# adaLN's later modulation vectors: transposed half rows of w_ada, multiplied with silu(c) and summed in one VectorE operation, in place of column sums that a matmul finishes

## The chip, the cores and the metric

The kernel runs on one core of a Trainium2 chip. The metric is the device time of one execution in microseconds (us); lower is better. The core's engines work in parallel, each through its own queue in order: TensorE (PE: matmuls, and their weight loads as PEld), VectorE (DVE), ScalarE (ACT), GpSimd (POOL), and SyncE (SP), whose queue issues every DMA of this kernel.

## The reference, cut to what matters

One layer of a hybrid encoder over a sequence of 1024 tokens with 1024 features, in float32. A conditioning vector `c` gives six modulation vectors, of which four are needed late: the gate of the attention part, shift and scale of the MLP part, and the gate of the MLP part.

```python
c_act = jax.nn.silu(c)                      # (1, 1024)
mod = c_act @ w_ada + b_ada                 # w_ada (1024, 6 * 1024)
shift_mix, scale_mix, gate_mix, shift_ffn, scale_ffn, gate_ffn = jnp.split(mod, 6, axis=-1)
h = modulate(rms_norm(x), shift_mix, scale_mix)          # h * (1 + scale) + shift
qa, ka, va, qb, kb, vb = jnp.split(h @ w_in, cuts, axis=-1)
oa = chunked_rel_attention(qa, ka, va, rel_bias)         # 8 heads
ob = stick_breaking_attention(qb, kb, vb)                # 8 heads
mixed = jnp.concatenate([rms_norm(oa) * g_a, rms_norm(ob) * g_b], axis=-1) @ w_out
x = x + gate_mix * mixed
h = modulate(rms_norm(x), shift_ffn, scale_ffn)
gate, val = jnp.split(causal_depthwise_conv(h @ w_up, conv_w, conv_b), 2, axis=-1)
x = x + gate_ffn * ((jax.nn.silu(gate) * val) @ w_down)
return rms_norm(x) * final_g
```

## The kernel before

Matrix products run as three matmuls each on a high and a low part of both operands (tiles ending in h and l); making the parts is work for ScalarE (the high part), VectorE and GpSimd (the low part, a subtraction).

The program has these stages. **Setup**, to about 75 us: the first two modulation vectors (`ada_sum`, with the features on the partitions), the modulated input `hT`, the first query and key products. **Attention**, to about 645 us: 128 units, each one head's 128 queries; units 0 to 63 are stick-breaking (pairs 0 to 3), units 64 to 127 chunked (pairs 4 to 7). A unit runs scores (matmuls `S`), weights (stick-breaking: ScalarE's sigmoids, a VectorE scan over `kt`, a GpSimd multiplication into `pb`; chunked: VectorE's maxima, ScalarE's exponential, a GpSimd scaling), transposes (matmuls `T`), the split of the transposed weights (ScalarE `pth`, VectorE `ptl`), and the product with the values (`pv`, again a `T` tile). Scores run two units ahead (`AHEAD`). Between the pieces `fill` puts matmuls `mm` of a list of jobs: the later projections and, at the end, the output projection of the stick-breaking half (`job_out_b`), which reads `w_out` and the first gate. **Output projection of the chunked half and the MLP** follow to the end.

The four later vectors are the generator `mods`, advanced once per unit from unit `MOD0` on. It takes 128 tiles `rawm` of 128 input features by 256 output features; a VectorE operation multiplies a tile with the 128 values of silu(c) that stand on its partitions and adds it to `macc`. After eight tiles the 128 partitions remain to be summed: `mod_out` does that with a matmul against ones, into a PSUM buffer of the tag "T" that attention uses too. The gates come out as a row and go through DRAM (`gate_d`), from which `load_gate` spreads them over all partitions; shift and scale come out as columns (`modv`).

The order in each queue is set by a scheduler, which places an instruction where its engine seems free, with the program's order as priority. TensorE's instructions of attention are pinned by `pe` (line 136) to the program's order, so that a matmul of `mod_out` holds its place among the others; the mods' VectorE operations and loads are not pinned. `BUFS` gives the buffers of each tag: `rawm` has 4 of 128x256, `macc` 1.

Of the kernel before, what the change touches and what calls it, by code (L numbers as in the profile page):

```python
# [11 lines left out]
F32 = mybir.dt.float32  # L12
# [35 lines left out]
MOD0 = 60  # L48
# [7 lines left out]
def build(nc, tc, t, ctx):  # L56
# [3 lines left out]
    def mk(pool, shape, dt, tag):  # L60
        cnt[0] += 1
        return pool.tile(shape, dt, name=f"{tag}_{cnt[0]}", tag=tag, bufs=BUFS.get(tag, 1))
# [16 lines left out]
    rev_d = mk(dr, [8, P, ULEN], F32, "revd")  # L79

# [54 lines left out]
    def pe(fn, *a, **k):  # L135
# [7 lines left out]
    smask = mk(pq, [P, P], F32, "smask")  # L143
    gp.memset(smask, 0.0)
    gp.affine_select(out=smask, in_=smask, pattern=[[-1, P]], compare_op=ALU.is_gt,
                     fill=NEG, base=0, channel_multiplier=1)
    smaskr, identr = (mk(pq, [P, P], F32R, n) for n in ("smaskr", "identr"))
    gp.tensor_copy(smaskr, smask)
# [63 lines left out]
    def new_k(pr):  # L212
        pr.kh = [mk(pq, [P, S], F32R, "kh") for _ in range(2)]
# [4 lines left out]
    ada = t["ada0"]  # L218
    sh_mix = mk(p0, [P, KB], F32, "sh_mix")
# [235 lines left out]
    sy.dma_start(rev_d, bass.AP(t["rev"].tensor, 0, [[ULEN, 8], [0, P], [1, ULEN]]))  # L455
    new_k(pairs[0])
# [88 lines left out]
    def job_out_b(_):  # L545
# [10 lines left out]
        bc = mk(p1, [P, S + 1], F32, "kt")  # L556
        load_gate(bc[:, 0:D])
# [331 lines left out]
    QC = 256  # L889

    def mods():


        seq = [(i, qt, kb) for i in MODS for qt in range(D // QC) for kb in range(KB)]
        tiles = {}

        def load(n):
            if n < len(seq):
                i, qt, kb = seq[n]
                tiles[n] = mk(p1, [P, QC], F32, "rawm")  # L900
                sy.dma_start(tiles[n], t["ada"][i - 2, kb, :, qt * QC:(qt + 1) * QC])

        load(0)
        load(1)
        yield
        for n, (i, qt, kb) in enumerate(seq):
            cols = i in (3, 4)
            if n % 2 == 0:
                load(n + 2)
                load(n + 3)  # L910
            w = tiles.pop(n)
            if kb == 0:
                if cols and qt == 0:
                    modv[i] = mk(p0, [P, KB], F32, f"mod{i}")
                acc = mk(p1, [P, QC], F32, "macc")
                ve.tensor_scalar(acc, w, cact[:, 0:1], None, ALU.mult)
            else:
                ve.scalar_tensor_tensor(acc, w, cact[:, kb:kb + 1], acc, ALU.mult, ALU.add)  # L918
            if kb == KB - 1:
                mod_out(i, qt, acc, cols)  # L920
            if n % 2:
                yield

    def mod_out(i, qt, acc, cols):
        mp = mk(ps1, [P, HALF], F32, "T")
        if cols:
            for b in range(2):
                pe(te.matmul, mp[:, b:b + 1], acc[:, b * P:(b + 1) * P], ones[:, 0:1], start=True, stop=True)
            k0 = 2 * qt
            ve.scalar_tensor_tensor(modv[i][:, k0:k0 + 2], mp[:, 0:2], 0.0 if i == 3 else 1.0,  # L930
                                    bada[:, 8 * i + k0:8 * i + k0 + 2], ALU.add, ALU.add)
        else:
            pe(te.matmul, mp[:, 0:QC], ones, acc, start=True, stop=True)
            bb = mk(p1, [1, QC], F32, "rawm")
            sy.dma_start(bb, bass.AP(t["b_ada"].tensor, i * D + qt * QC, [[QC, 1], [1, QC]]))
            ve.tensor_add(acc[0:1], mp[0:1, 0:QC], bb)
            sy.dma_start(gate_d[i // 5:i // 5 + 1, qt * QC:(qt + 1) * QC], acc[0:1])
# [583 lines left out]
```

## Time and profile before

| | |
|---|---|
| three runs | 1421.34, 1426.35, 1428.23 us; median 1426.35 us |
| profiled execution | 1425.51 us; its span, first to last instruction, 1423.5 us |
| TensorE busy | 1309.2 us (92% of the span) |
| VectorE busy | 1176.2 us (83%) |
| GpSimd busy | 864.9 us (61%) |
| ScalarE busy | 617.2 us (43%) |

Times in the views are from the span's start. Busy shares are averages over stages that differ; a stage is read by its own rows. In the views, L918 is line 918 of the kernel, `out<-in` names the tiles written and read, and "who waited" puts a wait down to the event that came last.

### The profile page before, as it was taken

To read this page: it belongs to the slowest core of one execution; us is meant where nothing else is said; L and a number is where in the kernel's file an instruction comes from. 1 tells how busy PE (TensorE), PEld (TensorE's weight loads), DVE (VectorE), ACT (ScalarE), POOL (GpSimd) and SP (SyncE) were. 2 spreads that over 40 slices of the span, in tenths; PEclk is the share of its full clock that TensorE was granted. 3 is DMA by queue.
4 is the path that set the end of the run, shared out by engine and by line. 5 is a ranking of instruction groups with operands and counts; after the bars stand their busy time and mean duration, and the time that the engine had idled before them with its cause. 6 is when DMAs were issued, how large, how long until landed. Compare 5 with 4: busy or idle time off the path is not lost.

```text
span 1423.5 us, 19845 instructions
## 1 busy us (share of the span) xinstructions
PE 1309.2 (92%) x6644; PEld 1083.0 (76%) x6644; DVE 1176.2 (83%) x1967; ACT 617.2 (43%) x1270; POOL 864.9 (61%) x760
## 2 busy tenths in 40 slices
PE   4889999999899978798887999999999999999996
PEld 2688998898778966676665877777777778777774
DVE  7858777677778868876889889999998889899887
ACT  5647567575545433333432333323333333333334
POOL 4646576765333436563578667776676677667664
PEclk9999999999999999899998999999999999999998
DMA  8534433414665686665011111111111111211213
GB/s 311 180 100 112 104 88 85 119 49 120 166 167 144 179 263 197 217 193 193 22 45 36 47 52 45 45 45 60 52 54 58 45 45 45 60 52 49 62 37 119
DMA packets 80047, 144.57 MB, mean 102 GB/s; under 512 B 10041, under 2 KB 36809, under 8 KB 79946
## 3 DMA queue, kind: packets, MB, share of 16 engines
q1 hardware_dynamic: 79946, 143.31, 33.9%
q8 instruction: 53, 0.87, 0.3%
q14 instruction: 48, 0.39, 0.1%
HBM read 102.89 MB, written 18.88 MB: 86 GB/s over the span
## 4 chain that ended last, share of the span: by engine, by line
PE 43%; DVE 35%; ACT 7%; issue 5%; DMA 5%; POOL 4%; SPq 1%; POOLq 0%; DVEq 0%; ACTq 0%
PE mm L136 14%; PE up L1128 12%; DVE y L1137 8%; PE T L136 6%; PE dnf L136 6%; DVE x L1262 4%; PE S L136 3%; ACT y L1133 3%; DVE ah L1071 3%; DVE y L1070 2%; DVE adaw L254 1%; DVE macc L918 1%; PE up L1302 1%; POOL wl L121 1%; DVE al L1072 1%
## 5 line engine op out<-in xcount | busy, mean ns | idle before, releaser
L1262 DVE TENSOR_TENSOR x<-dnf,x 128x512 f32<-128x512 f32 x340 | 222.5, 679 | 1.6 <-PE dnf L136 1.6
L1137 DVE SCALAR_TENSOR_TENSOR y<-y,sm,y 128x512 f32<-128x512 f32 (+2 forms) x160 | 187.3, 1171 | 28.8 <-ACT y L1133 28.7
L1128 PE MATMUL up<-h,wh 128*128 128x512 f32 x640 | 199.7, 393 | 2.6 <-ACT y L1170 1.8
L1094 POOL TENSOR_TENSOR wl<-raw,wh 128x1024 fp32r<-128x1024 f32 (+1 forms) x62 | 160.1, 2583 | 66.1 <-ACT wh L1092 59.5
L1133 ACT ACTIVATE y<-y,sm 128x512 f32<-128x512 f32 x80 | 65.3, 817 | 254.7 <-DVE y L1209 133.4
L136 PE MATMUL mm<-H,wh 128*128 128x512 f32 x448 | 150.2, 403 | 0.0
L1128 PEld LDWEIGHTS up<-h,wh 128*128 128x128 f32 x640 | 119.7, 189 | 31.1 <-ACT y L1170 5.2
L136 PE MATMUL dnf<-dh,ah 128*128 128x512 f32 x336 | 133.5, 397 | 10.0 <-DVE x L1262 8.8
L136 PE MATMUL dnf<-dl,ah 128*128 128x512 f32 x336 | 134.0, 399 | 3.7 <-POOL dl L1240 2.5
L802 POOL TENSOR_TENSOR pb<-pb,kt 128x512 f32<-128x512 f32 (+2 forms) x96 | 89.4, 945 | 77.0 <-DVE kt L799 50.0
L136 PE MATMUL dnf<-dh,al 128*128 128x512 f32 x336 | 132.6, 395 | 0.9 <-DVE al L1072 0.9
L1128 PE MATMUL up<-h,wl 128*128 128x512 f32 x320 | 125.3, 392 | 0.0
L822 DVE TENSOR_TENSOR ptl<-T,pth 128x512 fp32r<-128x512 f32 (+2 forms) x192 | 98.5, 517 | 30.7 <-ACT pth L821 29.0
L821 ACT CAST pth<-T 128x512 fp32r<-128x512 f32 (+2 forms) x192 | 87.4, 457 | 62.3 <-PE T L136 60.9
L795 POOL TENSOR_SCALAR pb<-pb,ri 128x640 f32<-128x640 f32 (+2 forms) x64 | 45.4, 711 | 106.2 <-DVE ri L794 67.7
L136 PE MATMUL mm<-wh,H 128*128 128x256 f32 x512 | 102.8, 292 | 6.6 <-DVE vs L511 6.6
L799 DVE TENSOR_TENSOR_SCAN kt<-kt 128x128 f32<-128x128 f32 (+3 forms) x64 | 98.2, 1534 | 9.8 <-ACT kt L784 9.4
L1128 PE MATMUL up<-Tc,wh 128*128 128x512 f32 x320 | 100.9, 396 | 4.6 <-ACT y L1154 4.5
L1240 POOL TENSOR_TENSOR dl<-modt,dh 128x512 fp32r<-128x512 f32 x42 | 65.3, 1554 | 64.3 <-ACT dh L1239 64.3
L1237 POOL TENSOR_TENSOR modt<-modt,modt 128x512 f32<-128x512 f32 x44 | 68.8, 1563 | 58.2 <-DMA modt<-w_down 58.2
L136 PE MATMUL S<-kh,qs 128*128 128x384 f32 (+5 forms) x352 | 99.5, 364 | 4.6 <-ACT pb L778 4.4
L136 PE MATMUL T<-ident,pb 128*128 128x128 f32 x528 | 91.1, 277 | 8.8 <-POOL pb L802 3.5
(214 smaller groups left out, 3451.1 us busy)
## 6 DMA issues: line engine op xcount, KB each, us to landing
raw<-w_up SPq DMA_DIRECT2D x44, 512.0 KB, 3.6
rawm<-ada SPq DMA_DIRECT2D x128, 128.0 KB, 2.4
qs<-ex SPq DMA_DIRECT2D x104, 128.0 KB, 2.5
modt<-w_down SPq DMA_DIRECT2D x44, 256.0 KB, 2.7
adaw<-ada SPq DMA_DIRECT2D x16, 512.0 KB, 5.7
raw<-w_qk SPq DMA_DIRECT2D x16, 512.0 KB, 3.6
kh<-ex SPq DMA_DIRECT2D x56, 128.0 KB, 2.6
tbd<-wh SPq DMA_DIRECT2D x18, 256.0 KB, 2.6
```

The lines of the kernel that those rows point to most:

```text
L136: r = fn(*a, **k)
L799: ve.tensor_tensor_scan(r, r, r, 1.0, ALU.mult, ALU.bypass)
L802: gp.tensor_mul(pt[:, a:b], pt[:, a:b], kt[:, a + 1:b + 1])
L821: sc.copy(dh, tp[:, 0:b - a])
L822: ve.tensor_sub(dl, tp[:, 0:b - a], f(dh))
L1094: late.append(lambda a=a, z=z: ko(gp.tensor_sub(wl[:, a:z], raw[:, a:z], f(wh[:, a:z]))))
L1128: ko(te.matmul(ps, w[x][:, kb], b[kb][y], start=start and n == 0, stop=n == 11, skip_group_check=True))
L1133: ko(sc.activation(y[:, a:z], src[:, a:z], AF.Identity, scale=cw[2][:, b], bias=cb[:, b]))
L1137: ko(ve.scalar_tensor_tensor(y[:, o:z], src[:, o - d:z - d], cw[2 - d][:, b], y[:, o:z], ALU.mult, ALU.add))
L1237: ko(gp.tensor_mul(raw, raw, gbc[hf]))
L1240: ko(gp.tensor_sub(wl, raw, f(wh)))
L1262: r = ve.tensor_add(xc, ps, xc)
```

## The change

The host hands in the four vectors' part of `w_ada` transposed, so that output features lie on the partitions and input features along a row. silu(c), which setup already has in every partition as `cbc`, is stored to DRAM (`c_d`) and its halves are loaded back as a tile `chalf` of 128x512. For each half, vector and block of 128 features, one VectorE `tensor_tensor_reduce` multiplies a 128x512 tile with `chalf` and sums along the row into one column of `asum`: 64 operations on 128x512 in place of 128 on 128x256, and no matmul. `mod_out` adds the two halves and the bias; a gate is stored to DRAM from the columns, 1024 single elements. `rawm` now has 2 buffers of 128x512, the same bytes as before; `chalf` has one buffer. A mask of setup moves into setup's pool, and `job_out_b` advances the generator until the first gate exists.

```diff
-    "pb": 3, ... "rawm": 4, "sq": 1, "msr": 2, "e0": 2,
+    "pb": 3, ... "rawm": 2, "sq": 1, "msr": 2, "e0": 2,
-MOD0 = 60
+MOD0 = 56
+    sy.dma_start(c_d, cbc[0:1])
...
         bc = mk(p1, [P, S + 1], F32, "kt")
+        while not gate_up:
+            next(bg)
         load_gate(bc[:, 0:D])
...
-        seq = [(i, qt, kb) for i in MODS for qt in range(D // QC) for kb in range(KB)]
-        tiles = {}
-
-        def load(n):
-            if n < len(seq):
-                i, qt, kb = seq[n]
-                tiles[n] = mk(p1, [P, QC], F32, "rawm")
-                sy.dma_start(tiles[n], t["ada"][i - 2, kb, :, qt * QC:(qt + 1) * QC])
+        seq = [(hf, n, kb) for hf in range(2) for n in range(len(MODS)) for kb in range(KB)]
+        tiles, ch = {}, {}
+
+        def load(x):
+            if x < len(seq):
+                hf, n, kb = seq[x]
+                cc = slice(hf * HALF, (hf + 1) * HALF)
+                if n == 0 and kb == 0:
+                    ch[hf] = mk(p1, [P, HALF], F32, "chalf")
+                    sy.dma_start(ch[hf], bass.AP(c_d.tensor, c_d.offset + hf * HALF, [[0, P], [1, HALF]]))
+                tiles[x] = mk(p1, [P, HALF], F32, "rawm")
+                sy.dma_start(tiles[x], t["ada"][n, kb, :, cc])
...
-                acc = mk(p1, [P, QC], F32, "macc")
-                ve.tensor_scalar(acc, w, cact[:, 0:1], None, ALU.mult)
-            else:
-                ve.scalar_tensor_tensor(acc, w, cact[:, kb:kb + 1], acc, ALU.mult, ALU.add)
+        for x, (hf, n, kb) in enumerate(seq):
+            load(x + 1)
+            w = tiles.pop(x)
+            ve.tensor_tensor_reduce(out=w, in0=w, in1=ch[hf], scale=1.0, scalar=0.0, op0=ALU.mult, op1=ALU.add,
+                                    accum_out=asum[:, hf, n, kb:kb + 1])
+            if hf and kb == KB - 1:
+                mod_out(n, MODS[n])
+            yield
...
-            pe(te.matmul, mp[:, 0:QC], ones, acc, start=True, stop=True)
-            bb = mk(p1, [1, QC], F32, "rawm")
-            sy.dma_start(bb, bass.AP(t["b_ada"].tensor, i * D + qt * QC, [[QC, 1], [1, QC]]))
-            ve.tensor_add(acc[0:1], mp[0:1, 0:QC], bb)
-            sy.dma_start(gate_d[i // 5:i // 5 + 1, qt * QC:(qt + 1) * QC], acc[0:1])
+    def mod_out(n, i):
+
+        v = modv[i] = mk(p0, [P, KB], F32, f"mod{i}")
+        ve.tensor_add(v, asum[:, 0, n], asum[:, 1, n])
+        ve.scalar_tensor_tensor(v, v, 1.0 if i == 4 else 0.0, bada[:, 8 * i:8 * i + KB], ALU.add, ALU.add)
+        if i in (2, 5):
+            sy.dma_start(bass.AP(gate_d.tensor, gate_d.offset + i // 5 * D, [[1, P], [P, KB]]), v)
+            gate_up.append(i)
...
-    ada = w6[:, :, 2:6].transpose(2, 0, 1, 3)
+    ada = w_ada[0].T.reshape(6, KB, P, D)[2:6]
```

What this does to the order is seen at three places. The first is TensorE's queue in the chunked stage, before: the last matmuls of a unit's product with the values (`T` from `pth` and `ptl`), then the matmul of `mod_out` on `macc`, then the next scores.

```order
L136 MATMUL T_4169<-pth_4061,vs_1713 128x128
L136 MATMUL T_4169<-ptl_4062,vs_1713 128x128
L136 MATMUL T_4203<-macc_3961,ones_70 128x256
L136 MATMUL S_4209<-kh_3150,qs_3825 128x256
L136 MATMUL S_4209<-kh_3150,qs_3826 128x256
```

And now, at the same place:

```order
L137 MATMUL T_4174<-pth_4072,vs_1716 128x128
L137 MATMUL T_4174<-ptl_4073,vs_1716 128x128
L137 MATMUL S_4205<-kh_3153,qs_3838 128x256
L137 MATMUL S_4205<-kh_3153,qs_3839 128x256
L137 MATMUL mm_4116<-wl_3146,H_113 128x256
```

The 16 places with `macc` are gone, and nothing else in TensorE's queue has moved. The second place is VectorE's queue in the second pair of the stick-breaking stage, around the scans of 896 and 1024 keys (`kt`), before:

```order
L799 SCALAR_TENSOR_TENSOR kt_1214<-kt_1214 128x896
L847 TENSOR_TENSOR o_1244<-T_1246,fx_1245 64x256
L822 TENSOR_TENSOR ptl_1264<-T_1261,pth_1263 128x128
L822 TENSOR_TENSOR ptl_1228<-T_1279,pth_1227 128x4x128
L799 SCALAR_TENSOR_TENSOR kt_1271<-kt_1271 128x1024
```

And now; the rows of `asum` alone are the read-out of the sum that belongs to the operation above each:

```order
L803 SCALAR_TENSOR_TENSOR kt_1217<-kt_1217 128x896
L917 ISA rawm_5100,asum_581<-rawm_5100,chalf_3691 128x512
L917 ISA asum_581 128x1
L851 TENSOR_TENSOR o_1247<-T_1249,fx_1248 64x256
L826 TENSOR_TENSOR ptl_1267<-T_1264,pth_1266 128x128
L917 ISA rawm_5130,asum_581<-rawm_5130,chalf_3691 128x512
L917 ISA asum_581 128x1
L826 TENSOR_TENSOR ptl_1231<-T_1282,pth_1230 128x4x128
L917 ISA rawm_5171,asum_581<-rawm_5171,chalf_3691 128x512
L917 ISA asum_581 128x1
L803 SCALAR_TENSOR_TENSOR kt_1274<-kt_1274 128x1024
```

All 64 sums now stand in VectorE's queue between rows that ran at 77 and 222 us before, nearly two for each unit; before, 8 of the 128 operations ran before 85 us and the other 120 from 347 us on. The third place is SP's queue at the same point, before: the store of a finished head pair, a weight load, and the copies of the next queries (`qs`).

```order
L857 DMA otld_58<-otl_1161 128x256
L126 DMA raw_1703<-w_qk 128x1024
L164 DMA qs_1302<-ex_1298 64x512
L167 DMA qs_1303<-ex_1298 64x512
L165 DMA qs_1302<-ex_1299 64x512
```

And now:

```order
L861 DMA otld_58<-otl_1164 128x256
L127 DMA raw_1706<-w_qk 128x1024
L910 DMA rawm_5100<-ada 128x512
L910 DMA rawm_5130<-ada 128x512
L910 DMA rawm_5171<-ada 128x512
L910 DMA rawm_5228<-ada 128x512
L910 DMA rawm_5292<-ada 128x512
L160 DMA qs_1305<-ex_1301 64x512
L163 DMA qs_1306<-ex_1301 64x512
```

Five loads, each of which has to wait for the sum that frees one of the two `rawm` buffers, now stand ahead of the copies of the queries.

## Rows read from the trace of the kernel before

**Rows 1.** Busy us of each engine by stretch, then clock, DMA share, GB/s.

```profile
core 0: us, PE busy (x) PEld busy (x) DVE busy (x) ACT busy (x) POOL busy (x), PEclk, DMA share, GB/s
77.00:222.00 145.00, 144.04 (x984) 132.77 (x984) 105.10 (x156) 91.50 (x226) 86.41 (x128) 0.99 0.35 91
...
357.00:440.00 83.00, 74.83 (x454) 65.44 (x453) 66.09 (x217) 41.25 (x115) 28.81 (x43) 0.96 0.60 164
440.00:500.00 60.00, 59.38 (x390) 53.35 (x389) 50.49 (x169) 30.87 (x92) 23.34 (x33) 1.00 0.60 166
500.00:645.00 145.00, 120.53 (x627) 98.47 (x626) 112.74 (x297) 47.93 (x142) 75.57 (x77) 0.93 0.70 215
...
720.00:1423.00 703.00, 666.79 (x2827) 529.76 (x2827) 625.32 (x776) 242.27 (x363) 482.86 (x281) 0.99 0.17 53
```

**Rows 2.** Same stretches, instructions with `macc` alone: PE, PEld, VectorE.

```profile
77.00:222.00 145.00, 0.00 (x0) 0.00 (x0) 3.84 (x7) 0.99 0.35 91
357.00:440.00 83.00, 2.35 (x12) 1.70 (x12) 21.51 (x43) 0.96 0.60 164
440.00:500.00 60.00, 2.12 (x16) 2.15 (x16) 17.26 (x32) 1.00 0.60 166
500.00:645.00 145.00, 4.71 (x16) 2.70 (x16) 29.64 (x44) 0.93 0.70 215
```

**Rows 3.** Waits of PE: 357 to 440 us, then 500 to 645 us.

```profile
PE S L136 <- ACT pb L778: 3.8, 3, 2.3
PE T L136 <- DVE macc L918: 3.1, 1, 3.1
...
PE T L136 <- DVE macc L918: 8.8, 2, 6.6
PE mm L136 <- DVE H L521: 6.1, 2, 3.6
```

**Rows 4.** The chain that ended last, by line: 357 to 440, then 500 to 645 us.

```profile
by line: PE mm L136 11.7%; issue 10.4%; DVE macc L918 10.0%; ACT pb L778 8.5%; PE T L136 6.0%; DVE S L771 5.7%; DVE nm L767 5.1%; DVE ptl L822 4.2%; PE S L136 4.0%; DMA gated<-macc 4.0%; DVE o L847 3.4%; DMA rawm<-ada 3.1%; DVE ex L175 2.8%
...
by line: PE mm L136 11.9%; issue 8.0%; DMA rawm<-ada 8.0%; DMA raw<-w_out 6.6%; PE T L136 6.1%; DVE macc L918 5.1%; DMA x<-tbd 4.8%; PE dn L136 3.8%; DVE ptl L822 3.4%; DMA tbd<-wh 3.4%; DVE H L521 3.3%; DVE wl L567 3.2%; POOL H L522 2.9%; 
```

**Rows 5.** Pieces of that chain, 500 to 645 us: start, length, what.

```profile
577.26 3.23 DMA gated<-macc
...
582.33 3.80 DMA rawm<-ada
```

**Rows 6.** Setup's sums with accumulator (ns min/median/max), and their read-outs.

```profile
L254 DVE CUSTOM_DVE_ANT_0 adaw<-adaw,cbc x16: 1209/1212/2309, 18.2 to 55.4; 128x1024 f32<-128x1024 f32 x16
L254 DVE DVE_READ_ACCUMULATOR2_ANT sh_mix<- x8: 76/78/83, 19.3 to 55.0; 128x1 f32 x8
```

**Rows 7.** VectorE addition with one input in SBUF: busy us, mean ns.

```profile
L1262 DVE TENSOR_TENSOR x<-dnf,x 128x512 f32<-128x512 f32 x340 | 222.5, 679 | 1.6 <-PE dnf L136 1.6
```

**Rows 8.** VectorE and GpSimd side by side: stick-breaking stage, `macc`, setup (ns min/median/max).

```profile
L855 DVE SCALAR_TENSOR_TENSOR otl<-o,sm,oth x15: 486/761/1019, 106.8 to 324.5; 128x256 fp32r<-128x256 f32 x15
...
L918 DVE SCALAR_TENSOR_TENSOR macc<-rawm,cact,macc x112: 414/485/1594, 76.9 to 620.0; 128x256 f32<-128x256 f32 x112
...
L307 POOL TENSOR_TENSOR H<-mod,H x14: 1264/2300/2341, 22.5 to 57.8; 128x512 fp32r<-128x512 f32 x14
```

**Rows 9.** VectorE's two-input operations, 77 to 222 us, by line: busy us, mean ns.

```profile
L799 DVE TENSOR_TENSOR_SCAN kt<-kt 128x128 f32<-128x128 f32 (+7 forms) x38 | 54.0, 1422 | 7.3 <-ACT kt L784 7.2
...
L855 DVE SCALAR_TENSOR_TENSOR otl<-o,sm,oth 128x256 fp32r<-128x256 f32 x8 | 5.6, 697 | 1.3 <-ACT oth L854 1.3
```

**Rows 10.** DMA issues: count, KB each, median us to landing; issue time (ns); the gate's reader.

```profile
modt<-w_down SPq DMA_DIRECT2D x44, 256.0 KB, 2.7
...
L901 SPq DMA_DIRECT2D rawm<-ada x128: 327/372/1951, 71.0 to 611.6; - x128
...
L543 SPq DMA_DIRECT2D kt<-gated x1: 320/320/320, 462.4 to 462.4; - x1
```

**Rows 11.** VectorE's waits, 500 to 645 us: total us, times, longest.

```profile
DVE macc L918 <- DMA rawm<-ada: 6.9, 5, 4.7
```

More of the change, by code (lines that the diff above doesn't have):

```diff
@@ L79, in build @@
     rev_d = mk(dr, [8, P, ULEN], F32, "revd")
+    c_d = mk(dr, [1, D], F32, "cd")
     c0, p0 = pool("p0", side="left")
@@ L142, in build @@
     lo64, hi64 = slice(0, HD), slice(HD, P)
[L143 to L146, printed above, removed]
     smaskr, identr = (mk(pq, [P, P], F32R, n) for n in ("smaskr", "identr"))
-    gp.tensor_copy(smaskr, smask)
     gp.tensor_copy(identr, ident)
@@ L218, in build @@
     ada = t["ada0"]
+    smask = mk(pst, [P, P], F32, "smask")
+    gp.memset(smask, 0.0)
+    gp.affine_select(out=smask, in_=smask, pattern=[[-1, P]], compare_op=ALU.is_gt,
+                     fill=NEG, base=0, channel_multiplier=1)
+    gp.tensor_copy(smaskr, smask)
     sh_mix = mk(p0, [P, KB], F32, "sh_mix")
@@ L887, in build @@
     modv = {}
-    QC = 256
+    asum = mk(p0, [P, 2, len(MODS), KB], F32, "asum")
+    gate_up = []
     def mods():
-        seq = [(i, qt, kb) for i in MODS for qt in range(D // QC) for kb in range(KB)]
-        tiles = {}
-        def load(n):
-            if n < len(seq):
-                i, qt, kb = seq[n]
-                tiles[n] = mk(p1, [P, QC], F32, "rawm")
-                sy.dma_start(tiles[n], t["ada"][i - 2, kb, :, qt * QC:(qt + 1) * QC])
+        seq = [(hf, n, kb) for hf in range(2) for n in range(len(MODS)) for kb in range(KB)]
[9 more added lines that the diff above has]
+                sy.dma_start(tiles[x], t["ada"][n, kb, :, cc])
@@ L903, in mods @@
         load(0)
-        load(1)
         yield
[L906 to L914, printed above, removed]
-                acc = mk(p1, [P, QC], F32, "macc")
-                ve.tensor_scalar(acc, w, cact[:, 0:1], None, ALU.mult)
-            else:
-                ve.scalar_tensor_tensor(acc, w, cact[:, kb:kb + 1], acc, ALU.mult, ALU.add)
[L919 to L932, printed above, removed]
-            pe(te.matmul, mp[:, 0:QC], ones, acc, start=True, stop=True)
-            bb = mk(p1, [1, QC], F32, "rawm")
-            sy.dma_start(bb, bass.AP(t["b_ada"].tensor, i * D + qt * QC, [[QC, 1], [1, QC]]))
-            ve.tensor_add(acc[0:1], mp[0:1, 0:QC], bb)
-            sy.dma_start(gate_d[i // 5:i // 5 + 1, qt * QC:(qt + 1) * QC], acc[0:1])
+        for x, (hf, n, kb) in enumerate(seq):
[6 more added lines that the diff above has]
+            yield
```

2 rows, old and new, of the table BUFS are left out of this document.

## Prediction

> **What bounds the kernel now.** I read the busy times by stretch first [rows 1], because the shares over the whole span hide that the stages differ. From 77 to 222 us, the first pairs of stick-breaking attention, TensorE is busy 144.04 of 145 us while VectorE has about 40 us free: TensorE is the bound there. In the chunked stage it is not. From 357 to 440 us TensorE is idle for 8.2 us, and from 500 to 645 us for 24.5 of 145 us; only 440 to 500 us is full (59.38 of 60). After 720 us the change touches nothing: 666.79 of 703 us busy.
>
> The second view asks how much of this is the mods' work [rows 2]: 21.51 us of VectorE and 2.35 us of TensorE in 357 to 440 us, 17.26 and 2.12 us in 440 to 500, 29.64 and 4.71 us in 500 to 645, against 3.84 and none in 77 to 222. So nearly all of it lies where TensorE waits. The third view names waits [rows 3]: TensorE stands 3.1 and 8.8 us directly before a matmul on `macc`. These understate, since VectorE's queue is in order and the maxima for the next exponentials stand behind a `macc` operation too; the 3.8 us for ACT `pb` are partly of that kind. The fourth view, the chain that ended last, counts such steps [rows 4]: in 357 to 440 us `macc` operations hold 10.0%, the store of a gate 4.0% and the loads of `rawm` 3.1% of it; in 500 to 645 us loads hold 8.0% and operations 5.1%, with single steps of 3.8 us, and a gate's store of 3.23 us [rows 5].
>
> **What the change removes.** In 357 to 440 us the three shares are 17.1% of 83, 14.2 us. TensorE cannot finish earlier than its own work allows: its idle 8.2 us and the removed 2.35 us are 10.5 us [rows 1, 2]. I take 10.5. In 440 to 500 us TensorE is full, so only the matmuls go: 2 us. In 500 to 645 us 13.1% of 145 are 19.0 us, with the gate's store 22.2 us; TensorE's idle and removed time would allow 29.2. I take 22, because the waits of 6.1 us for `w_out`'s parts [rows 3] stay and are late next. Together 34.5, rounded to **35 us gained**. The bounds: only the waits that name `macc`, 11.9 us, and 9.2 us of matmuls give 21; all idle time of the three stretches, 33.3 us, and the matmuls give 42.
>
> **What it moves.** The 64 new sums are no longer held by a pinned matmul, and the order puts all of them into VectorE's queue at what was 77 to 222 us, where TensorE is full and has no idle time to give. There is no 128x512 sum with accumulator in the trace; setup has the same operation on 128x1024, 1212 ns, with a read-out of 78 ns [rows 6]. Beside it stands a 128x512 addition that takes one input from SBUF, 679 ns [rows 7]; 512 elements more cost 533 ns. So the new sum takes 0.68 us and 0.08 us for its read-out, 0.76 us with nothing in its way.
>
> Beside GpSimd's work such operations are stretched. In the stick-breaking stage the 128x256 operation `otl`, both tensors in SBUF as for the new sum, has a minimum of 486 ns [rows 8] and a mean of 697 ns [rows 9]: 0.21 us more. I take 0.97 us for a sum, 62 us for 64, and 1 us for the eight small additions. VectorE then needs 105.10 - 3.84 + 62 + 1 = 164.3 us in a stretch of 145 [rows 1, 2]. It becomes the bound, and its queue is in order, so the scan and the low parts `ptl` behind a sum are late, and TensorE's pinned transposes and value products with them: 19.3 us. Without any stretching the 64 sums take 48.4 us, and the excess is 6.
>
> Two more costs belong to the same stretch. A sum waits for its load, and with two buffers a load waits for the sum two places ahead. One round is the issue, 0.37 us, the landing of 256 KB, 2.7 us [rows 10], and the sum, 0.97: 4.0 us for two sums, 129 us for 64. That fits into 145 us on average but not in each place, as five loads in a row on SP's queue show, with the copies of the next queries behind them. Before, VectorE waited 6.9 us for `rawm` around 44 operations [rows 11], 10 us for 64; half of it should fall into time in which VectorE would have waited for ScalarE anyway, which leaves 5. `chalf` has one buffer, so its second half is loaded only after the 32nd sum: about 3 us, of which I take 2. Together **26 us lost**.
>
> **What costs nothing.** The store of a gate from columns, 1024 elements of 4 bytes, has no like in the trace; its landing could take far longer than the store of a row and be hidden still, for the first gate is read only at 462 us [rows 10] and its store now stands in the order before what ran at 222 us. If it were late, `job_out_b` would wait. The store of silu(c), the mask's new place and the loop in `job_out_b` add no work to an engine at a place where another waits for it; `MOD0` changes the priority only.
>
> **The sum.** The profiled execution took 1425.51 us: 1425.51 - 35 + 26 = 1416.5. It lies 0.84 us below the median of the three runs, so against that median I predict **1417 us**, 0.65% less. About 0.5% (7 us) is what a measurement of this kernel can tell from no change.
>
> **A rule weighed.** Setup's row shows that GpSimd's 128x512 subtraction took 1264 ns alone and 2300 ns in the median, while the sums beside it mostly kept 1212 ns [rows 6, 8]: one engine waits while the other works. The Trainium skill ("SBUF — State Buffer", section "SBUF: two separate sides") says that VectorE operations with two SBUF inputs and GpSimd share one pair of ports, which the one that starts first keeps for its whole instruction. By that rule the trace agrees, and it speaks against this place for the sums: the second rival below is what it would do here.
>
> A second rule, the Trainium skill's "Vector Engine (DVE) Microarchitecture Reference" (section "Points that are easy to get wrong"), has an accumulating operation with two fp32 inputs from SBUF run at half rate. The trace disagrees: 1024 elements with accumulator took 1212 ns, and 512 without one 679 ns [rows 6, 7], the same rate. Still it is the third rival.
>
> **Rivals.**
> 1. *The two halves cancel.* The chain loses the `macc` steps, but the next path, `w_out`'s loads and the exponentials, ends only a little earlier (gain 25), and the loss is 26: 1426 us. For it: `issue` and ACT `pb` already hold 10.4% and 8.5% of the chain [rows 4]. Against it: with a quarter of VectorE's time in `macc` [rows 2], 440 to 500 us shows that chunked units can keep TensorE full.
> 2. *Slower: VectorE and GpSimd take turns in the stick-breaking stage.* If their two-input work excludes each other, the stretch must hold GpSimd's 86.41 us [rows 1], the scans' 54.0 and `otl`'s 5.6 us [rows 9] and 43.5 us of sums: 189.5 in 145, 44 us lost. With 35 gained that is 1435 us. It decides the sign once the loss exceeds 35 us. For it speaks GpSimd's 2300 ns; against it, that the 86.41 us contain waiting already, and that a scan and the GpSimd work that follows it mostly alternate by their data anyway.
> 3. *Slower: half rate.* A 512-wide sum would then cost what 1024 elements cost now, 1.21 us, and with read-out and stretching 1.5 us: 96 us for 64, an excess of 53 and with the waits 60 us: 1451 us.
> 4. *The sums vanish.* They fill VectorE's idle 40 us, with 6 us of excess, and the chunked stage gains 35: 1397 us. Against it: TensorE at 144.04 of 145 us has nothing to absorb a late scan.
> 5. *The change does not do what it says.* It does: the rows of the order show the matmuls gone. That their removal gains nothing would need the waits on `macc` to be replaced one for one; the 9.2 us of matmuls alone speak against it.
>
> **How the numbers follow.** I give the forecast 0.36 (1405 to 1421), rival 1 0.24, rival 2 0.22, rival 3 0.03, rival 4 0.13, rival 5 0.02. Faster by over 0.5% are most of the forecast's case, rival 4, and hardly any of rival 1: 0.47. Within 0.5% are rival 1, rival 5 and the edges of the forecast and of rival 2: 0.28. Slower is the rest: 0.25. Gain 42 with loss 6 would be 1390 us, gain 21 with loss 44 would be 1449 us; the range takes in 8 in 10 between them, 1394 to 1444. The forecast's own range is 1405 to 1421.
>
> **What the profile after will show.** If I am right: no `macc`, no matmul against ones on it; 64 sums of 0.7 to 1.1 us, all before the chunked stage; TensorE clearly below full in the first pairs, waiting for the scans' products and `ptl`, and VectorE above 90% busy there; the whole stick-breaking stage some 26 us longer; the chunked stage, from the first chunked scores to about the first output-projection `dn`, some 35 us shorter, with TensorE nearly full to about where `w_out` is first loaded. Wrong would be: sums of 1.2 us or more; GpSimd operations stretched to twice their minimum and waited for by TensorE; VectorE idle before sums for `rawm` in total above 10 us, which would mean that two buffers, not VectorE's time, set the pace; or a chunked stage in which TensorE waits as much as before for ScalarE's exponentials.

## The result, and the profile after

The changed kernel takes 1440.46 us (median of four, 1439.46 to 1440.58) against 1423.85 us beside it: the ratio is 1.0112, 95% interval [1.0081, 1.0143]. It is slower by 1.1%, where 1417 us, 0.65% faster, was predicted. The profiled execution took 1439.46 us, its span 1437.3. The ratios and intervals, here and below, leave out two slow executions: 3193 us of the kernel before and 5232 us of e14.

First the stretches of [rows 1], after the change: us, then busy us (and count) of PE, PEld, DVE, ACT, POOL, clock, DMA share, GB/s.

```profile
77.00:222.00 145.00, 115.93 (x707) 100.81 (x706) 106.45 (x202) 64.57 (x165) 67.40 (x95) 0.91 0.51 147
222.00:320.00 98.00, 85.75 (x528) 75.19 (x527) 79.15 (x123) 57.01 (x134) 59.81 (x79) 0.96 0.46 123
...
357.00:440.00 83.00, 78.45 (x505) 70.29 (x505) 59.88 (x162) 50.24 (x128) 44.93 (x63) 0.98 0.37 92
440.00:500.00 60.00, 59.74 (x397) 53.91 (x396) 42.46 (x152) 35.64 (x106) 22.82 (x35) 1.00 0.42 105
500.00:645.00 145.00, 135.63 (x783) 115.62 (x781) 101.87 (x311) 63.42 (x189) 78.89 (x90) 0.96 0.61 183
```

From 77 to 222 us TensorE has lost 28 us of work, 144.04 to 115.93, with a mean granted clock of 0.91 between its two levels of 1.2 and 2.4 GHz, 0.99 before. VectorE has not become full: it is busy 106.45 us in place of 105.10, although 47 of the 64 sums lie here. So it waits. In the three later stretches TensorE works 3.6, 0.4 and 15.1 us more, though a stretch of fixed times no longer holds the same work as before.

The stages are better cut by an operation than by a time. `S<-S,kt` prepares a chunked unit's scores; its first one marks the end of the stick-breaking stage, its last one the end of the chunked stage (columns: count, ns min/median/max, first and last start in us, forms). Before:

```profile
L771 DVE CUSTOM_DVE_ANT_0 S<-S,kt x64: 285/432/433, 332.9 to 626.8; 128x256 f32<-128x256 f32 x56, 128x128 f32<-128x128 f32 x8
```

After:

```profile
L775 DVE CUSTOM_DVE_ANT_0 S<-S,kt x64: 289/432/433, 384.9 to 641.7; 128x256 f32<-128x256 f32 x56, 128x128 f32<-128x128 f32 x8
```

The stick-breaking stage ends 52.0 us later. The chunked stage takes 256.8 us in place of 293.9, a gain of 37.1. The rest to the end takes 795.6 us in place of 796.7. 52.0 - 37.1 - 1.1 = 13.8 us, the difference of the two spans.

The same cut for the engines, from 77 us to the first `S<-S,kt` and from there to the last (columns as above). Before:

```profile
77.00:332.90 255.90, 250.72 (x1665) 227.84 (x1665) 187.84 (x267) 164.73 (x394) 165.39 (x235) 0.99 0.35 91
332.90:626.80 293.90, 261.61 (x1548) 226.27 (x1547) 237.48 (x725) 129.75 (x376) 131.25 (x163) 0.95 0.63 182
```

After:

```profile
77.00:384.90 307.90, 265.16 (x1666) 233.96 (x1665) 233.41 (x394) 162.87 (x393) 171.01 (x234) 0.95 0.46 126
384.90:641.70 256.80, 244.15 (x1499) 214.06 (x1498) 178.69 (x587) 128.33 (x375) 124.01 (x163) 0.97 0.52 147
```

In the stick-breaking stage TensorE's idle time rises from 5.2 to 42.7 us. That is 37.6 us of the 52.0. The other 14.4 us are busy time: as many matmuls as before take longer, at a mean granted clock of 0.95 in place of 0.99. In the chunked stage its idle time falls from 32.3 to 12.7 us, by 19.6. Of the 17.5 us less busy time there, 10.5 are the matmuls on `macc`; the other 7.0 are shorter matmuls, at a clock of 0.97 in place of 0.95.

The waits after, 77 to 275 us (engine, line, what is waited for; us in total, times, longest):

```profile
POOL pb L806 <- DVE kt L803: 64.1, 19, 9.7
DVE rawm L917 <- DMA rawm<-ada: 39.6, 23, 8.0
...
PE T L137 <- DVE ptl L826: 25.6, 14, 8.8
```

Before, in the same stretch:

```profile
POOL pb L802 <- DVE kt L799: 37.2, 18, 7.6
```

VectorE stands 39.6 us before sums whose load has not landed. Its queue is in order, so the scan `kt` and the low parts `ptl` behind the sum are late; GpSimd waits for the one, TensorE's transposes and products for the other (1.7 us in the whole stage before). SyncE's own queue in the same stretch waits in turn for VectorE:

```profile
SPq L910 <- DVE asum L917: 68.3, 30, 11.6
```

The two queues hold each other up: a load stands at SyncE until the sum two places ahead has freed its buffer, a sum stands at VectorE until the load has landed. The chain that ended last, 77 to 275 us, answers to [rows 4]: by line, then pieces (start, length, what).

```profile
by line: DMA rawm<-ada 35.1%; DVE kt L803 15.1%; DVE rawm L917 13.7%; issue 9.1%; DVE ptl L826 8.2%; PE mm L137 3.3%; POOL pb L806 2.4%; DVE o L851 2.2%; POOL wl L122 2.1%; DVE otl L859 1.7%; ACT kt L788 1.1%; ACT pth L825 1.1%; PE T L137 1
...
87.15 2.58 DMA rawm<-ada
89.87 0.69 DVE rawm L917
90.60 3.01 DMA rawm<-ada
...
168.82 7.44 DMA rawm<-ada
...
202.15 12.60 DMA rawm<-ada
```

Loads hold 35.1% of the chain, the sums 13.7%. The first three pieces are the plain round: a load of 2.6 to 3.0 us, a sum of 0.69, the next load. The load at 168.82 us follows the second load of `chalf`; the one at 202.15 us follows the first store of a gate (issues of line 929, then their time to landing; the trace has a landing for the second store alone, 11.1 us):

```profile
L929 SPq DMA_DIRECT2D gated<-mod x2: 377/382/387, 201.5 to 273.5; - x2
...
DMA to landing us min/median/max: 11.1/11.1/11.1
```

The sums themselves and their read-outs, the answer to [rows 6]:

```profile
L917 DVE CUSTOM_DVE_ANT_0 rawm<-rawm,chalf x64: 660/693/1582, 77.3 to 271.1; 128x512 f32<-128x512 f32 x64
L917 DVE DVE_READ_ACCUMULATOR2_ANT asum<- x64: 75/80/88, 78.5 to 271.7; 128x1 f32 x64
```

### The profile page after: what moved, and what is told of

Same layout as the page of the kernel before. It is cut to its first block, busy times and chain, and to the rows that moved or that the text cites. A ratio compares the mean times of both kernels' runs of the same rounds, so it can differ in the third digit from the quotient of the medians.

```text
span 1437.3 us, 19575 instructions
## 1 busy us (share of the span) xinstructions
PE 1310.6 (91%) x6596; PEld 1078.6 (75%) x6596; DVE 1165.8 (81%) x1959; ACT 614.8 (43%) x1270; POOL 865.5 (60%) x760
## 4 chain that ended last, share of the span: by engine, by line
DVE 39%; PE 37%; ACT 7%; DMA 6%; issue 5%; POOL 5%; SPq 0%; DVEq 0%; POOLq 0%; ACTq 0%
PE up L1121 13%; PE mm L137 11%; DVE y L1130 9%; PE dnf L137 6%; PE T L137 5%; DMA rawm<-ada 5%; DVE x L1255 4%; ACT y L1126 3%; DVE ah L1064 3%; DVE kt L803 3%; PE S L137 2%; DVE y L1063 2%; DVE rawm L917 2%; DVE ptl L826 2%; DVE adaw L255 1%
## 5 line engine op out<-in xcount | busy, mean ns | idle before, releaser
L806 POOL TENSOR_TENSOR pb<-pb,kt 128x512 f32<-128x512 f32 (+2 forms) x96 | 93.6, 989 | 113.7 <-DVE kt L803 84.5
L137 PEld LDWEIGHTS T<-ident,pb 128*128 128x128 f32 x528 | 66.4, 143 | 54.7 <-issue 20.7
```

Of the source, the lines that this page charges most:

```text
L137: r = fn(*a, **k)
L806: gp.tensor_mul(pt[:, a:b], pt[:, a:b], kt[:, a + 1:b + 1])
```

## The experiments

Four theories stood behind them. **A**: the loads set the pace, since two buffers and two queues in order leave a load no head start. **B**: VectorE's added work at this place is the loss, and the waits only fill what it would lose anyway. **C**: the gate's store of single elements is part of it. **D**: the place is the cost, since the matmuls that held the mods back are gone. The table gives for each kernel the median, the ratio to the kernel before beside it with its interval, the first and last `S<-S,kt` of the profiled execution, what that makes of the stick-breaking (SB) and the chunked stage against before, and VectorE's waits for `rawm` in total. The last three columns come from one execution each, which lay between 2.7 us below its kernel's median (e4) and 5.8 us above it (e9), so a few us between two stages tell nothing.

| kernel | us | ratio [95%] | first, last | SB, chunked | waits |
|---|---|---|---|---|---|
| changed | 1440.46 | 1.0112 [1.0081, 1.0143] | 384.9, 641.7 | +52.0, -37.1 | 39.6 |
| e1 no loads | 1408.93 | 0.9892 [0.9868, 0.9916] | 358.5, 610.7 | +25.6, -41.7 | 0.7 |
| e2 gate in runs | 1431.84 | 1.0049 [1.0032, 1.0067] | 378.3, 636.3 | +45.4, -35.9 | 31.7 |
| e3 loads held, from unit 56 | 1433.11 | 1.0060 [1.0033, 1.0088] | 337.2, 634.1 | +4.3, +3.0 | 39.8 |
| e4 before, no matmul | 1438.05 | 1.0101 [1.0073, 1.0130] | 381.7, 639.3 | +48.8, -36.3 | 10.9 |
| e5 sums held, from unit 56 | 1412.60 | 0.9902 [0.9877, 0.9927] | 333.8, 615.6 | +0.9, -12.1 | 3.4 |
| e6 over 128 units | 1413.11 | 0.9907 [0.9889, 0.9924] | 339.6, 612.6 | +6.7, -20.9 | 4.6 |
| e7 units 0 to 63 | 1416.01 | 0.9932 [0.9910, 0.9954] | 365.0, 617.6 | +32.1, -41.3 | 16.7 |
| e8 four small buffers | 1440.00 | 1.0097 [1.0075, 1.0119] | 383.6, 642.1 | +50.7, -35.4 | 18.4 |
| e9 two, no chalf | 1426.25 | 1.0012 [1.0000, 1.0023] | 376.5, 634.0 | +43.6, -36.4 | 27.7 |
| e10 three, no chalf | 1424.45 | 1.0002 [0.9992, 1.0013] | 369.7, 626.8 | +36.8, -36.8 | 16.5 |
| e11 e3, gate in runs | 1417.90 | 0.9964 [0.9949, 0.9979] | 338.9, 624.1 | +6.0, -8.7 | 28.0 |
| e12 48 and 16 | 1419.11 | 0.9966 [0.9956, 0.9976] | 358.9, 621.7 | +26.0, -31.1 | 14.2 |
| e13 units 0 to 63, no loads | 1403.21 | 0.9862 [0.9835, 0.9889] | 351.2, 604.3 | +18.3, -40.8 | 0 |
| e14 units 0 to 63, three | 1408.19 | 0.9891 [0.9860, 0.9921] | 355.4, 612.4 | +22.5, -36.9 | 1.6 |

**e1, no loads.**

```diff
-                tiles[x] = mk(p1, [P, HALF], F32, "rawm")
-                sy.dma_start(tiles[x], t["ada"][n, kb, :, cc])
+                if x < 2:
+                    tiles[x] = mk(p1, [P, HALF], F32, "rawm")
+                    sy.dma_start(tiles[x], t["ada"][n, kb, :, cc])
+                else:
+                    tiles[x] = tiles[x - 2]
```

> The changed kernel with only the first two tiles of w_ada loaded; the 64 sums read and write these two over and over, so 62 loads are left out and the four vectors are not the layer's. Theory A (the loads set the pace: two buffers, SyncE's queue in order, VectorE's queue in order): VectorE's idle time for rawm, 39.6 us in the changed kernel, is gone, the loss of about 52 us in the stick-breaking stage falls to 10 to 20 us, the gain of 37 us stays: 1400 to 1412 us. Theory B (VectorE's added work at this place is the cost, the waits only fill what it would lose anyway): the loss stays at 40 us or more: 1428 us or more.

Measured 1408.93 us, 31.5 less than the changed kernel. The loss in the stick-breaking stage falls from 52.0 to 25.6 us, so 26.4 us of it go with the loads; A's 10 to 20 is missed by 6 us, and B's 40 by more. Both have a part, and the two are not cleanly apart, since without loads the order set the sums still denser, all between 77 and 177 us:

```profile
L920 DVE CUSTOM_DVE_ANT_0 rawm<-rawm,chalf x64: 657/686/1576, 77.7 to 176.1; 128x512 f32<-128x512 f32 x64
```

The busy times of this kernel in these 100 us and in the 45 after them (columns as above):

```profile
77.00:177.00 100.00, 80.76 (x468) 69.17 (x468) 98.02 (x202) 44.07 (x108) 54.77 (x65) 0.90 0.32 67
177.00:222.00 45.00, 45.00 (x308) 41.35 (x307) 34.48 (x52) 30.50 (x76) 25.42 (x39) 1.00 0.28 68
```

Here VectorE is full, 98.02 of 100 us, and TensorE is at 80.76; it is full again as soon as the sums are over.

**e2, the gate in runs.** Each partition writes 8 neighbouring elements.

```diff
-            sy.dma_start(bass.AP(..., gate_d.offset + i // 5 * D, [[1, P], [P, KB]]), v)
+            sy.dma_start(bass.AP(..., gate_d.offset + i // 5 * D, [[KB, P], [1, KB]]), v)
```

> The changed kernel with each gate stored as 128 runs of 32 bytes in place of 1024 single elements; the gate's features are thereby permuted. Theory C (the store of single elements blocks the load behind it and costs what VectorE then idles before sum 44, about 8 us): 1430 to 1434 us, landing of the load behind the store under 5 us in place of 12.6. If that idle time lies beside other waits: 1438 to 1441 us, unchanged.

Measured 1431.84 us, 8.6 less, as C says; the load behind the first store landed after 2.7 us in place of 12.6. The landing of the second store in this kernel:

```profile
DMA to landing us min/median/max: 1.4/1.4/1.4
```

The store takes 1.4 us in place of 11.1, VectorE's waits for `rawm` fall by 7.9 us, the longest from 8.0 to 5.6. From e5 on, the kernels get the same runs by another order of the gates' features in `ada` and in the bias, so that nothing is permuted in the result.

**e4, the kernel before without its matmuls.**

```diff
-            pe(te.matmul, mp[:, 0:QC], ones, acc, start=True, stop=True)
...
-            ve.tensor_add(acc[0:1], mp[0:1, 0:QC], bb)
+            ve.tensor_add(acc[0:1], acc[0:1], bb)
```

> The kernel before with the matmuls of mod_out left out: row 0 of macc, not summed over the partitions, goes on as the vector, so the four vectors are not the layer's. Theory D says that those matmuls, fixed in TensorE's order, held the mods back: without them the 128 operations on macc, 0.5 us each, move into the stick-breaking stage, and the kernel is slower than before by 5 us or more: 1430 us or more, though it has less work. Rival (the matmuls are only work and waits): 9 to 12 us are saved: 1413 to 1417 us.

Measured 1438.05 us, slower by 1.0% with less work. The 112 operations on `macc` moved:

```profile
L918 DVE SCALAR_TENSOR_TENSOR macc<-rawm,cact,macc x112: 452/485/1365, 76.7 to 303.8; 128x256 f32<-128x256 f32 x112
```

Before, they ran to 620.0 us [rows 8]. So the fixed matmuls held the mods at their place, and taking them away alone gives nearly the whole result: +48.8 and -36.3 us, where the change has +52.0 and -37.1. That the two are so near does not make them the same loss: up to its first `S<-S,kt` VectorE is busy 258.01 us in e4 and 233.41 in the changed kernel, and it waits 10.9 us for `rawm` in e4, 39.6 there. The old form costs more work, the new one more waits.

**e3, loads held at their place, from unit 56 on.** `ko` keeps an instruction behind the one written ahead of it on its engine.

```diff
-                sy.dma_start(tiles[x], t["ada"][n, kb, :, cc])
+                ko(sy.dma_start(tiles[x], t["ada"][n, kb, :, cc]))
```

> The changed kernel with the loads of rawm and chalf held in the program's order of SyncE's queue, so that the sums run one per unit from unit 56 on, nearly all in the chunked stage, where VectorE has idle time. Theory D (the place is the cost, the new form itself is cheaper: 49 us of VectorE in place of 68, and 9 us of matmuls less): the stick-breaking stage is as long as before, the chunked one 10 to 25 us shorter: 1400 to 1416 us. Rival (a load round through two buffers costs the same anywhere, and the held loads stop the other transfers behind them): the chunked stage is as long as before or longer: 1425 to 1445 us.

Measured 1433.11 us: the rival. The stick-breaking stage is as before but for 4.3 us, and the chunked stage gains nothing. The chain from 440 to 500 us in this kernel shows why:

```profile
446.80 5.83 DMA rawm<-ada
...
461.76 3.08 DMA rawm<-ada
...
479.48 11.36 DMA gated<-mod
...
492.92 4.44 DMA rawm<-ada
```

The gate's store again, now directly ahead of its reader, and the loads, held behind stores that wait for a finished head pair; TensorE is busy 48.68 of these 60 us, 59.38 before.

**e11, the same with the gate in runs.**

> The kernel with held loads from unit 56 on, and a gate stored in runs of 32 bytes. If the 10.7 us that TensorE lost from 440 to 500 us there were the store of single elements: 1419 to 1425 us, and VectorE's longest wait for rawm under 7 us in place of 12.3. If it was the place of the held loads alone: 1430 us or more.

Measured 1417.90 us, just below the first range: 15.2 less than e3, by the two ratios 14. The longest wait for `rawm` is 5.0 us. The store was it, and more than the 10.7 us.

**e5, the sums held in place of the loads.**

```diff
-            ve.tensor_tensor_reduce(out=w, in0=w, in1=ch[hf], ...)
+            ko(ve.tensor_tensor_reduce(out=w, in0=w, in1=ch[hf], ...))
```

> The changed kernel with two edits: the sums themselves, not their loads, are held in the program's order on VectorE (one per unit from unit 56 on), and the gates' features lie so over partitions and columns that a gate is stored in runs of 32 bytes. The loads may go ahead as far as two buffers allow. The kernel with held loads lost 10.7 us of TensorE's work from 440 to 500 us to the first gate's store, which landed just when it was needed. If that store and the loads' place in SyncE's queue are what remained: 1405 to 1418 us. If two buffers cost the chunked stage its waits wherever the loads stand: 1422 to 1432 us.

Measured 1412.60 us, within the first range, and faster than the kernel before by 1.0%. The loads may now be issued as soon as a buffer is free, ahead of the stores. VectorE's waits over the stage:

```profile
DVE rawm L917 <- DMA rawm<-ada: 3.4, 3, 2.9
```

3.4 us in place of e11's 28.0, and 5.3 us less time, by the two ratios 9. e5 and e6 are the fastest kernels with the whole computation here; 1412.60 and 1413.11 us cannot be told apart.

**e6 and e7, other paces.** Sums and loads both held; e6 advances the generator at every second unit from 0, e7 at every unit from 0 on (`MOD0 = 0`).

```diff
-        if i >= MOD0:
+        if i >= 0 and i % 2 == 0:
             next(bg, None)
```

> As the kernel before it, but sums and loads are both held in the program's order, one sum every second unit from unit 0 to unit 126: 32 in the stick-breaking stage, 32 in the chunked one, each with a load issued one sum (about 8 us) ahead. Theory A (only the load round in the way of VectorE's queue costs): waits for rawm under 8 us in all, 1398 to 1412 us. Theory B (each sum in the stick-breaking stage delays a scan by its 0.77 us, since TensorE is full there): 32 sums lose up to 25 us and the gain of the chunked stage is 20 to 37: 1413 to 1430 us.

> As the kernel before it, but one sum per unit from unit 0 to unit 63: all 64 in the stick-breaking stage, evenly over its 250 us, as in the changed kernel but at half the density, one load of 2.7 us per unit of 4 us. The chunked stage then keeps its whole gain of about 37 us. Theory A: waits for rawm under 15 us, loss in the stick-breaking stage 10 to 20 us: 1398 to 1410 us. Theory B (the sums' own 49 us are lost there): 1430 us or more.

e6 took 1413.11 us, at the border of both ranges: 4.6 us of waits and 6.7 us lost, but only 20.9 gained. e7 took 1416.01 us, between the two: 16.7 us of waits, just over A's bound, and 32.1 us lost, over A's 20. D in its strict form is gone: with its sums still early, e7 is 24 us faster than the changed kernel, some 9 of them by the gate's store as in e2, and faster than the kernel before.

**e8, four buffers of half the size**, in the changed kernel's free order.

```diff
-    ..., "rawm": 2, ...
+    ..., "rawm": 4, ...
...
-        seq = [(hf, n, kb) for hf in range(2) ...]
+        seq = [(hf, n, kb) for hf in range(4) ...]
```

> The changed kernel in its own free order, with a gate stored in runs of 32 bytes, but quarter rows: 128 sums on 128x256 and four buffers of rawm, loads three ahead, chalf of 256 columns loaded four times. The same bytes are in flight as with two buffers of 512, in smaller pieces, and VectorE has 64 more operations and read-outs, about 14 us more work. Theory A: waits for rawm fall by half, and this about pays for the additional work: 1424 to 1434 us. Theory B (VectorE's work is what is lost): 1440 us or more.

Measured 1440.00 us, B's bound. The waits fell from e2's 31.7 to 18.4 us for `rawm` and 5.1 for `chalf`; the sums' busy time rose from 56.7 to 73.9 us, that of the read-outs from 5.1 to 10.2. So 22 us more work and 8 us fewer waits cost 8 us against e2: VectorE's work is not free in this stretch, though it is not full.

**e9 and e10, a third buffer in the free order.**

```diff
-            ve.tensor_tensor_reduce(out=w, in0=w, in1=ch[hf], ...)
+            ve.tensor_tensor_reduce(out=w, in0=w, in1=w, ...)
```

and for e10

```diff
-    ..., "rawm": 2, ...
+    ..., "rawm": 3, ...
...
-            load(x + 1)
+            load(x + 2)
```

> The changed kernel in its free order, a gate stored in runs of 32 bytes, and each sum multiplying its tile with itself, not with chalf: silu(c) is left out, chalf and its two loads are gone, and the four vectors are not the layer's. Two buffers as in the change. It is the base for the next kernel. Theory A: only the wait at the second half's load of chalf, 5.7 us, goes: 1424 to 1430 us, waits for rawm 24 to 30 us.

> The same with three buffers of rawm, which chalf's room allows, and loads two ahead. Theory A (two buffers are too few: a load's landing of 2.7 us stands behind every second sum): waits for rawm under 12 us, the last scans 10 us or more earlier than with two: 1410 to 1420 us. Rival (the loads wait for their place in SyncE's queue, not for a buffer): waits above 20 us, 1424 us or more.

e9 took 1426.25 us, 5.6 less than e2, as expected. e10 took 1424.45 us, only 1.8 less than e9, with 16.5 us of waits: A's numbers missed, the rival's met by the time alone. The stage looks 6.8 us shorter, but e9's profiled execution lay 5.8 us above its median and e10's 0.7 below. Here a third buffer also let the order set the sums closer, the last one at 217.9 us in place of 261.3.

**e12, three quarters early.** 48 sums in units 0 to 63, 16 after, both held.

```diff
+        if 0 <= i < 64 and i % 4 != 3 or i >= 64 and i % 4 == 0:
```

> The kernel with 64 sums over 128 units, sums and loads held, but 48 of them in the stick-breaking stage (three in four units) and 16 in the chunked one (one in four). In the even spread 32 sums lengthened the stick-breaking stage by 6.7 us, 0.2 us each, and the chunked one by 21 us against none there, 0.65 us each. If these prices hold: 6 to 9 us less than the even spread, 1404 to 1408 us. If the price in the stick-breaking stage rises with the density (0.5 us each for 64 sums there): 1411 to 1416 us.

Measured 1419.11 us, above both ranges: 26.0 us lost for 48 sums, with 14.2 us of waits. That is 0.54 us for each early sum, where e6 has 0.21 for 32 and e7 0.50 for 64. The price rises from every second unit to three in four, and no further.

**e13 and e14, one sum per unit without loads, and with three buffers.** e13 is e7's place with e1's edit, the sums held; e14 is e7 with e10's edits.

> One sum per unit from unit 0 to 63, sums held in the program's order, but only the first two tiles of w_ada loaded, as in the first experiment (62 loads are left out, the four vectors are not the layer's). The first experiment, without loads but with all sums between 77 and 177 us, still lost 25.6 us in the stick-breaking stage. If that was density (more VectorE work than those 100 us hold): the loss falls to 5 to 12 us over the 250 us of the stage, 1390 to 1398 us. Rival (every sum in that stage costs about 0.4 us, since it stands ahead of a scan in VectorE's queue): the loss stays at 20 to 26 us, 1404 to 1411 us.

> One sum per unit from unit 0 to 63, sums and loads held, each tile multiplied with itself (silu(c) and chalf left out), three buffers of rawm and loads two sums ahead, about 8 us. With two buffers and loads one ahead the same pace had waits of 16.7 us and lost 32.1 us. Theory A (the load's head start decides, not the number of operations): waits under 6 us, loss 12 to 22 us, 1396 to 1407 us. Rival (the loads' place in SyncE's queue decides): waits above 12 us, 1412 us or more.

e13 took 1403.21 us: the loss of 25.6 us fell to 18.3 at the slower pace, so 7 us of it were density (by the two ratios 4), and 18.3, 0.29 us for each sum, stay; neither range is met. e14 took 1408.19 us, 1.2 us above A's range, and lost 22.5 us, 0.5 more than A's bound, in place of e7's 32.1; the waits are 1.6 us in place of 16.7. At one and the same pace a load that starts two sums ahead takes the waits away, and 10 us of the stage's loss with them; the whole kernel gains 7.8 us, by the two ratios 6. That is A, but for what `chalf`, which e14 leaves out too, cost e7: the wait before e7's 33rd sum, the first with the second half, is 1.75 us.

## Why the prediction was wrong

**The gain was right.** Predicted 35 us, measured 37.1. The reason held for most of it: 19.6 us less idle time of TensorE and 10.5 us of matmuls on `macc`. The last 7.0 us, shorter matmuls at a higher granted clock, stood in no term; that the sum came so near is in part luck.

**The loss was twice what was predicted.** Predicted 26 us, measured 52.0, and that turned the sign. The mechanism stood in the text, and also the sign to look for: VectorE idle before sums for `rawm` in total above 10 us, "which would mean that two buffers, not VectorE's time, set the pace". It was 39.6 us. By its terms:

- *A sum takes 0.97 us with its read-out.* Right: the mean was 0.906 and 0.08 us. The stretching by GpSimd is there too (below).
- *VectorE overfull, 19.3 us.* Near in size: 25.6 us without loads in a denser order, where VectorE was full, and 18.3 us at one per unit. But with the loads VectorE never came to be full; "above 90% busy" was wrong. And it need not be full to cost something: in e13 it is busy 119.48 of the 145 us, and TensorE still falls from 144.04 to 138.25:

```profile
77.00:222.00 145.00, 138.25 (x911) 124.49 (x911) 119.48 (x198) 85.64 (x209) 97.81 (x122) 0.97 0.32 83
```

  That fits a queue in order, in which a scan that has become ready stands behind a sum, whatever idle time VectorE has elsewhere; it was not tried apart from the other causes (Open).
- *Load waits, 5 us, and `chalf`, 2 us.* This is the step that failed: it has 7 us, and the next one none, where the runs put 26.4 us on the loads, 8.6 of them by the gate's store. Its sentence was that a round of 4.0 us for two sums, 129 us in all, "fits into 145 us on average". The sums took from 77.3 to 271.1 us, 6 us for two. By the trace's times, a load was issued 1.0 us in the mean after its buffer came free: 43 of 62 within 0.1 us, the other 19 after 0.6 to 6.1 us behind other transfers in SyncE's queue. The sum began 4.3 us after the issue, where 3.1 was counted, since some loads landed late (behind the gate's store after 12.6 and 11.7 us) and some sums whose load had landed stood behind other work on VectorE. With 0.9 us for sum and read-out that is 6.2. That half of the waits would fall into VectorE's other waits was a guess that no row bore out.
- *The gate's store "costs nothing".* Wrong, 8.6 us (e2). The text asked only whether its reader would be late; the loads behind it on the same queue were.
- *No term: TensorE's matmuls.* The loss was counted as idle time alone. 14.4 of the 52.0 us are matmuls that took longer at the lower mean granted clock; every difference between runs above holds a part of them.

Against 26 us too little, the runs thus have 8.6 us for the store, 11 us more for the loads and `chalf` than the 7 that were counted, and 6 us more for the sums. The ladder of runs splits the load part: the changed kernel 1440.46 us, with the gate in runs 1431.84 (8.6), without `chalf` 1426.25 (5.6), without loads 1408.93 (17.3); by the ratios 9, 5 and 17. Together they are 31 us of time, 26.4 of them in the stick-breaking stage. The last two are not one edit apart, since e1 keeps `chalf` and the single elements, behind which none of its loads stands.

**The rivals.** None came as written. Rival 2's 1435 us is the nearest number, by luck: it has 44 us of turns and no waits for loads. But the turns have a part. In the changed kernel the 29 sums beside which GpSimd ran no two-tensor operation took 679 to 695 ns, the 35 others 1084 ns in the mean and up to 1582: 13.8 us of VectorE's time, by the trace's times, near the 13.4 us that the prediction's 0.21 for each of 64 make. GpSimd's products on 128x512 took 1180 ns in the mean from 77 to 222 us before and 1249 in the changed kernel, its low parts `wl` 913 and 982. They are stretched most in e13, which has the sums at an even pace beside them (out<-in, count, busy us, mean ns, idle us before them):

```profile
L806 POOL TENSOR_TENSOR pb<-pb,kt 128x512 f32<-128x512 f32 x24 | 30.9, 1296 | 22.4 <-DVE kt L803 14.9 <-ACT kt L788 4.0 <-PE T L137 1.9
L122 POOL TENSOR_TENSOR wl<-raw,wh 128x256 fp32r<-128x256 f32 x26 | 27.2, 1075 | 0.1
```

In e13 GpSimd is busy 97.81 us in the stretch, 86.41 before, and the rival's 44 us are not there: e13 lost 18.3 in all. How much of that is the turns, no run shows. Half rate: 512 elements took 693 ns in the median, as [rows 6, 7] had it. The sums did not vanish, and the two halves did not cancel.

**The place.** That the order would take the sums early was read from the order. e4 shows that the missing matmul did it, and e5, that with the sums held late the change is worth 1.0%, with sums of 57.3 us and read-outs of 5 on VectorE in place of 78.3 us of operations on `macc`, and without 10.5 us of matmuls. How the 1.0% falls to these two is not shown: no kernel holds the old form late without its matmuls. Held early at an even pace it is worth 0.7% (e7). What the change lacked is a place for its sums and a head start for its loads.

**Open.** Why a third buffer in the free order gave 1.8 us and not more is argued from the closer order of the sums, not tried by itself: no kernel has three buffers and e9's order. Whether the 0.29 us per sum of e13 are late scans, late `ptl`, GpSimd's stretched work or longer matmuls was not tried apart. In that stage TensorE waits 10.1 us for `pb`, 3.5 before, and 4.2 us for `ptl`, 1.7 before; so GpSimd's product, which comes after the scan, is the larger part of its idle time. Whether the lower clock follows from the idle time alone was not tried either.

## What to carry to other kernels

An instruction that is fixed in one queue can be the brake that holds free ones in others at a good place: before it is removed, look where they go, and hold them there by themselves. A round of load and use through two buffers is to be compared with the gaps in the queues that it passes, place by place, not with the stage's total; what it costs is what stands behind the waiting instruction on an engine in order. The four kernels with an even pace and under 5 us of waits (e5, e6, and with part of the work left out e13 and e14) took 1403 to 1413 us, whether their sums stood early or late.

## What the runs showed of the hardware

A store of 1024 single elements of 4 bytes (the second gate's) landed after 11.1 us, and after 12.7 us in e3; the same 4 KB in 128 runs of 32 bytes landed after 1.4 us in e2. It does not hurt its reader alone: the load issued right behind the first gate's store on the same queue landed after 12.6 us, where the median of these loads is 2.8. The Trainium skill ("DMA: Bandwidth & Descriptors", section "Specifications", the row on the minimum transfer for line rate) has transfers below 512 bytes off the full rate. Both stores are below it, and between them lies a factor of 8 in these runs; no run here has the same store in runs of 512 bytes or more.
